# Two stacked transformer blocks on one core: what stands at the borders of stages, and on which engine

## The chip, the cores and the metric

The kernel runs on one core of a Trainium2 chip. The metric is device time in microseconds of one whole launch. The engines named below are TensorE (PE: products; its weight loads are PEld), VectorE (DVE), ScalarE (ACT), GpSimd (POOL) and SyncE (SP, which issues the weights' transfers here). Each engine works through its own list of instructions in order.

## The reference, cut to what matters

The input is one sequence of 512 tokens with 1024 features. A block of two layers is followed by a second block. Every stage has the same frame: a norm over the features, a mixer or a feed-forward, a residual.

```python
def first_block(x, c, ...):
    cond = jax.nn.silu(c)
    for layer in range(2):
        mod = cond @ ada_w[layer] + ada_b[layer]
        sh1, sc1, g1, sh2, sc2, g2 = jnp.split(mod, 6, axis=-1)
        h = modulate(rms_norm(x), sh1, sc1)          # rms_norm(x) * (1 + sc) + sh
        y = pool_attention_mixer(h, ...) if layer % 2 == 0 else mlstm_mixer(h, ...)
        x = x + g1[:, None, :] * y
        h = modulate(rms_norm(x), sh2, sc2)
        x = x + g2[:, None, :] * swiglu(h, ffn_w1[layer], ffn_w3[layer], ffn_w2[layer])
    return x
```

The second block goes on with x: `x + 0.5 * swiglu_2(rmsnorm(x))` (ffn1), a mixer of two kinds of heads (mixer2), attention of 4 heads to 256 memory rows, which have a norm, keys and values of their own (mem), `x + 0.5 * swiglu_2(rmsnorm(x))` again (ffn2), and a last norm with gains. `swiglu` is `(silu(h @ w1) * (h @ w3)) @ w2` with 2816 hidden features.

## The kernel before, in words

**Data.** x lies transposed, as 8 tiles of 128 features x 512 tokens. Every product is made in three passes of a short float format: a value is split into a high half (`wh`, `xh`) and the rest (`wl`, `xl`), and `mm3` (L160 to L162) adds wh·xh, wh·xl and wl·xh. A product here is one such pass, 128x128 by 128x512 or 128x256.

**Weights.** A block of 128 output columns comes by DMA into `raw` (SyncE, pool `rp`, two buffers of 256 columns). ScalarE copies it to `wh` (L151), VectorE subtracts to get `wl` (L130). The pool `wp` holds two `wh` and two `wl`, so at most two blocks are prepared at any time; a third waits until the products have finished with the first.

**A projection** (`proj`) goes over 8 output tiles: 8 steps of 3 products each fill one PSUM tile, then `evac` adds it to x (`resid`, L824, or L819 and L820 where the norm's factor is still to be applied), and `ss_add` squares the new tile (ScalarE) and adds it to `ssq` (GpSimd, L300 and L302). Behind the eighth tile two products with a matrix of ones (L305, L306) sum over the partitions, and `rsqrt` makes `rstd` from that: Ln and Exp on ScalarE, then four VectorE operations of a Newton step (L322 to L325).

**The norm's use.** In the first block the tiles x·(1+sc) are made ahead (`mod_pre`, GpSimd, L431). Once `rstd` is there, `modulated` (L441 to L443) multiplies by it, adds the shift and splits; `modulated_forms` (L452) does the same and goes on to the sums that the feed-forward of layer 1 needs. Four of the eight multiplications are on GpSimd (`modpool`), four on VectorE. In the second block rstd is applied to the results instead, so the products need not wait for it.

**The feed-forwards** `ffn` (layer 1, ffn1, ffn2) work in three groups of 8, 8 and 6 hidden tiles. A group is a row of units, each with seven 128x256 products per step (`uprod` 1 to 7, L562 to L564), made of sums of blocks of the weights (`usums`, `ublocks`, `usums2` on VectorE: L530, L531, L547, L548) and of x (`lead`, `trail`, L502). A unit gives gated values `g`. At the end of a group the 8 output tiles are computed from the group's `g`. Tile 0's products with the values that exist already, and then tile 1's, are issued ahead of those with the last two values, which are just being made; they fill that time. `ffn_plain` (layer 0) is the ordinary form. `mem_kv` makes keys and values of the memory (L250 to L252 or L160 to L162) at three borders: half of the keys behind pool attention's projection, half behind ffn0, the values behind the mLSTM's projection.

**Order.** A scheduler lays the program out on the engines by the order in the code, by dependences and by when buffers come free in its own estimate; what it decides is fixed before the run.

## Time and profile before

| | us |
|---|---|
| median of 3 runs (lowest, highest) | 2502.51 (2501.54, 2503.48) |
| the profiled execution, its own time | 2500.92 |
| its span in the trace | 2498.9 |
| PE busy | 2391.6 |
| DVE busy | 1832.5 |
| ACT busy | 1170.7 |
| POOL busy | 331.7 |
| mean granted clock of PE | 0.985 |

The span is the time from the first to the last instruction in the trace. Busy times are sums over instructions, and matmuls are pipelined, so a busy PE isn't yet a PE at its full pace. The granted clock says which share of full speed the chip let PE have: 1.00 is 2.4 GHz, 0.50 is 1.2.

### The profile page before, as it was taken

The numbers are of one execution on the slowest core, as the hardware profiler recorded it, in microseconds if no ns is written. First come the engines' busy times: TensorE is split into PE (matmuls) and PEld (weight loads), VectorE is DVE, ScalarE is ACT, GpSimd is POOL, SyncE is SP. The second block draws the span as 40 slices with busy tenths as digits, with TensorE's granted clock in tenths as the row PEclk, the third lists the DMA queues.
The fourth block names the chain that finished last, engine by engine and source line by source line (L and its number), as shares of the span: only waits on it lengthen the run. The fifth ranks groups of instructions, "written<-read, shape, count | busy, mean of one in ns | idle before, by whom it ended". The sixth has DMA issues, their size and how long they took to land.

```text
span 2498.9 us, 35096 instructions
## 1 busy us (share of the span) xinstructions
PE 2391.6 (96%) x13914; PEld 2068.8 (83%) x13914; DVE 1832.5 (73%) x2914; ACT 1170.7 (47%) x1880; POOL 331.7 (13%) x364
## 2 busy tenths in 40 slices
PE   7898999999999998999998999999999999999997
PEld 5567788888788668989898999988888787889896
DVE  6888765746777758857579777775778756978786
ACT  3562322222457736535366444444555545645453
POOL 1334100002212341000001000011011401000003
PEclk9999999999999999999999999999999999999999
DMA  9417564634333224333322333322111221233332
GB/s 297 132 58 229 160 219 132 212 112 152 98 112 97 82 85 127 110 101 103 101 86 85 102 102 102 102 92 84 51 51 51 85 87 58 93 102 102 102 98 72
DMA packets 265852, 276.25 MB, mean 111 GB/s; under 512 B 6588, under 2 KB 258364, under 8 KB 265688
## 3 DMA queue, kind: packets, MB, share of 16 engines
q1 hardware_dynamic: 265688, 274.02, 34.4%
q8 instruction: 109, 1.79, 0.3%
q14 instruction: 55, 0.45, 0.1%
HBM read 268.47 MB, written 5.53 MB: 110 GB/s over the span
## 4 chain that ended last, share of the span: by engine, by line
PE 73%; DVE 15%; ACT 5%; issue 4%; DMA 2%; POOL 1%; DVEq 0%; SPq 0%; ACTq 0%; POOLq 0%
PE ps L160 13%; PE ps L162 13%; PE ps L161 13%; PE ps L562 9%; PE ps L564 9%; PE ps L563 9%; DVE wl L130 2%; ACT wh L151 1%; DVE acc L388 1%; DVE qk L1059 1%; DMA rb<-rd 1%; PE ps L250 1%; PE ps L252 1%; PE ps L251 1%; DVE u L502 1%
## 5 line engine op out<-in xcount | busy, mean ns | idle before, releaser
L151 ACT ACTIVATE wh<-raw 128x1024 fp32r<-128x1024 f32 (+1 forms) x326 | 336.1, 1032 | 663.7 <-PE ps L161 488.7
L130 DVE TENSOR_TENSOR wl<-raw,wh 128x1024 fp32r<-128x1024 f32 (+1 forms) x326 | 404.8, 1242 | 72.2 <-ACT wh L151 67.4
L160 PE MATMUL ps<-h,wh 128*128 128x512 f32 x1040 | 417.9, 404 | 2.6 <-ACT wh L151 1.6
L162 PE MATMUL ps<-h,wl 128*128 128x512 f32 x1040 | 409.4, 395 | 6.6 <-DVE wl L130 6.6
L161 PE MATMUL ps<-h,wh 128*128 128x512 f32 x1040 | 412.1, 397 | 1.5 <-DVE h L852 1.2
L162 PE MATMUL ps<-g,wl 128*128 128x512 f32 (+1 forms) x780 | 297.4, 381 | 8.9 <-DVE wl L130 8.9
L160 PE MATMUL ps<-g,wh 128*128 128x512 f32 (+1 forms) x780 | 299.1, 383 | 4.5 <-DVE x L824 2.4
L161 PE MATMUL ps<-g,wh 128*128 128x512 f32 (+1 forms) x780 | 295.7, 379 | 0.0
L162 PEld LDWEIGHTS ps<-h,wl 128*128 128x128 f32 x1040 | 196.7, 189 | 52.9 <-DVE wl L130 9.1
L160 PEld LDWEIGHTS ps<-h,wh 128*128 128x128 f32 x1040 | 197.6, 190 | 45.8 <-ACT wh L151 3.6
L161 PEld LDWEIGHTS ps<-h,wh 128*128 128x128 f32 x1040 | 197.3, 190 | 45.1 <-DVE h L852 2.9
L563 PE MATMUL ps<-h,wh 128*128 128x256 f32 x726 | 206.4, 285 | 0.0
L151 ACT ACTIVATE c<-ps 128x256 f32<-128x256 f32 (+1 forms) x288 | 108.6, 385 | 172.7 <-PE ps L564 161.6
L162 PEld LDWEIGHTS ps<-g,wl 128*128 128x128 f32 x780 | 148.2, 190 | 40.7 <-DVE wl L130 14.0
L160 PEld LDWEIGHTS ps<-g,wh 128*128 128x128 f32 x780 | 148.4, 190 | 32.9 <-issue 4.3
L562 PE MATMUL ps<-h,wh 128*128 128x256 f32 x594 | 169.9, 286 | 3.1 <-ACT h L151 1.8
L161 PEld LDWEIGHTS ps<-g,wh 128*128 128x128 f32 x780 | 148.3, 190 | 28.0 <-issue 1.5
L564 PE MATMUL ps<-h,wl 128*128 128x256 f32 x594 | 168.6, 284 | 0.0
L388 DVE SCALAR_TENSOR_TENSOR acc<-araw,cond,acc 128x256 f32<-128x256 f32 x315 | 154.3, 508 | 5.4
L300 POOL COPY ssq<-sq 128x512 f32<-128x512 f32 x8 | 7.7, 958 | 1108.8 <-ACT sq L151 1108.8
L563 PEld LDWEIGHTS ps<-h,wh 128*128 128x128 f32 x726 | 140.5, 194 | 0.3 <-issue 0.2
L562 PE MATMUL ps<-hx,wh 128*128 128x256 f32 x462 | 132.8, 288 | 2.2 <-ACT wh L151 2.0
(451 smaller groups left out, 5690.6 us busy)
## 6 DMA issues: line engine op xcount, KB each, us to landing
raw<-in_ffn_w_dram SPq DMA_DIRECT2D x60, 1024.0 KB, 5.3
araw<-in_ada_w_dram SPq DMA_DIRECT2D x48, 1024.0 KB, 5.2
raw<-in_ffn_w_gu_dram SPq DMA_DIRECT2D x44, 1024.0 KB, 5.1
raw<-in_ffn_w_down_dram SPq DMA_DIRECT2D x16, 1024.0 KB, 5.1
raw<-in_w_in_dram SPq DMA_DIRECT2D x14, 1024.0 KB, 5.0
raw<-in_od_w_in_dram SPq DMA_DIRECT2D x12, 1024.0 KB, 5.5
raw<-in_mem_w_kv_dram SPq DMA_DIRECT2D x8, 1024.0 KB, 6.9
raw<-in_ffn_w_dram SPq DMA_DIRECT2D x8, 768.0 KB, 4.4
```

Source lines behind the costliest of these rows:

```text
L130: nc.vector.tensor_tensor(out=lo, in0=src, in1=hi.bitcast(F32), op=ALU.subtract)
L151: r = nc.scalar.activation(out=out, in_=in_, func=func, **kw)
L160: mm(out, wh, xh, start=first, stop=False)
L161: mm(out, wh, xl, start=False, stop=False)
L162: mm(out, wl, xh, start=False, stop=last)
L250: mm(out, xh[:, sl], wh[:, k], start=(half == 0 and i % 2 == 0 and k == 0), stop=False)
L251: mm(out, xl[:, sl], wh[:, k], start=False, stop=False)
L252: mm(out, xh[:, sl], wl[:, k], start=False, stop=(half == 1 and i % 2 == 1 and k == 3))
L388: nc.vector.scalar_tensor_tensor(out=acc, in0=tk, scalar=self.cond[:, k:k + 1], in1=acc, op0=ALU.mult, op1=ALU.add)
L562: mm(out, wh[:, k], xh, start=(m in (1, 5) and k == 0), stop=False, skip_group_check=True)
L563: mm(out, wh[:, k], xl, start=False, stop=False, skip_group_check=True)
L564: mm(out, wl[:, k], xh, start=False, stop=(k == 3), skip_group_check=True)
```

## The change

It has five parts. (1) GpSimd's work at the borders moves: the additions to `ssq` to VectorE (the first square is written there directly by ScalarE), `mod_pre`, the gains of the last norm and the high halves of the memory rows to ScalarE, the four multiplications with `rstd` to VectorE. (2) The two products with ones and `rsqrt` become `ss_fin` and are issued later: behind the first tile of `mem_kv`, behind product 1 of the first unit of a feed-forward, inside the first tiles of mixer2 and of the memory's queries. (3) The next stage's first weights are loaded and split beside the projection ahead: `unit_steps` and `weight_steps` hang on the tiles of that projection; the first unit of each group has a raw buffer of its own, `ur`. (4) `mem_kv` becomes a generator that is issued in turns with `modulated` or `modulated_forms` (`beside`). (5) At the end of a group tile 1 is issued ahead with 3 steps instead of `gn - 2`.

```diff
-    modpool, outpool = (2, 4, 5, 7), (1, 3)
+    outpool = (1, 3)
...
+    def begin(self, w, c0, ncol, step):
+
+        if step == 0:
+            self.eraw = self.raw(w, 0, KT, c0, ncol)
+        else:
+            self.esplit = self.wsplit(self.eraw[:, :, 0:P])
+
+    def raw(self, w, k0, nk, c0, ncol, t=None):
+
+        if self.esplit and self.eraw is not None:
+            v, self.eraw = self.eraw, None
+            return v
+        if t is None:
+            t = self.rp.tile([P, 2048], F32, tag="raw", name=self.nm("raw"))
         v = t[:, 0:nk * ncol].rearrange("p (k c) -> p k c", k=nk)
         self.nc.sync.dma_start(
...
     def wsplit(self, v):
+        if self.esplit:
+            v, self.esplit = self.esplit, None
+            return v
...
     def ss_add(self, src):
 
-        nc = self.nc
-        w = src.shape[-1]
-        sq = self.np.tile([P, S], F32, tag="sq", name=self.nm("sq"), bufs=3)[:, 0:w]
-        self.act(out=sq, in_=src, func=AF.Square)
         n = self.ssn
         self.ssn += 1
         if n == 0:
-            self.ssq = self.np.tile([P, S], F32, tag="ssq", name=self.nm("ssq"))[:, 0:w]
-            nc.gpsimd.tensor_copy(out=self.ssq, in_=sq)
-        elif n < KT - 1:
-            nc.gpsimd.tensor_tensor(out=self.ssq, in0=self.ssq, in1=sq, op=ALU.add)
-        if n == KT - 1:
-            self.ssp = self.ps("ss")
-            nc.tensor.matmul(self.ssp[:, 0:w], self.tab("ones"), self.ssq, start=True, stop=False)
-            nc.tensor.matmul(self.ssp[:, 0:w], self.tab("ones"), sq, start=False, stop=True)
-            self.rstd = self.rsqrt(self.ssp[:, 0:w], 1.0 / D, self.np, "rstd")
+            self.ssq = self.np.tile([P, S], F32, tag="ssq", name=self.nm("ssq"))
+            self.act(out=self.ssq, in_=src, func=AF.Square)
+            return
+        sq = self.np.tile([P, S], F32, tag="sq", name=self.nm("sq"), bufs=3)
+        self.act(out=sq, in_=src, func=AF.Square)
+        if n < KT - 1:
+            self.nc.vector.tensor_tensor(out=self.ssq, in0=self.ssq, in1=sq, op=ALU.add)
+        else:
+            self.sslast = sq
+
+    def ss_fin(self):
+
+        mm = self.nc.tensor.matmul
+        ssp = self.ps("ss")
+        mm(ssp, self.tab("ones"), self.ssq, start=True, stop=False)
+        mm(ssp, self.tab("ones"), self.sslast, start=False, stop=True)
+        self.ssn = 0
+        self.rstd = self.rsqrt(ssp, 1.0 / D, self.np, "rstd")
+        return self.rstd
...
     def mod_pre(self, layer, which, k, tag=None):
 
         pre = self.h(F32) if tag is None else self.t(tag=tag)
-        self.nc.gpsimd.tensor_scalar(out=pre, in0=self.x[k], scalar1=self.mod_cols(layer, which, k)[1], scalar2=0.0,
-                                     op0=ALU.mult, op1=ALU.add)
+        self.act(out=pre, in_=self.x[k], func=AF.Copy, scale=self.mod_cols(layer, which, k)[1])
         return pre
 
-    def modulated(self, layer, which, pres):
+    def modulated(self, layer, which, pres, hs):
+
         nc = self.nc
-        hs = []
         for k, pre in enumerate(pres):
             sh = self.mod_cols(layer, which, k)[0]
             xh, xl = self.h(), self.h()
-            (nc.gpsimd if k in self.modpool else nc.vector).tensor_tensor(out=pre, in0=pre, in1=self.rstd, op=ALU.mult)
+            nc.vector.tensor_tensor(out=pre, in0=pre, in1=self.rstd, op=ALU.mult)
             self.act(out=xh, in_=pre, func=AF.Identity, bias=sh)
             nc.vector.scalar_tensor_tensor(out=xl, in0=pre, scalar=sh, in1=xh.bitcast(F32), op0=ALU.add,
                                            op1=ALU.subtract)
             hs.append((xh, xl))
-        return hs
-
-    def modulated_forms(self, layer, which, pres):
-
-        nc, fs = self.nc, []
+            yield
...
+    def modulated_forms(self, layer, which, pres, fs):
+
         for k, pre in enumerate(pres):
-            (nc.gpsimd if k in self.modpool else nc.vector).tensor_tensor(out=pre, in0=pre, in1=self.rstd, op=ALU.mult)
+            self.nc.vector.tensor_tensor(out=pre, in0=pre, in1=self.rstd, op=ALU.mult)
             self.act(out=pre, in_=pre, func=AF.Identity, bias=self.mod_cols(layer, which, k)[0])
             if k % 2 == 0:
                 fs.append(self.lead(pre))
             else:
                 self.trail(fs[-1], pre)
-        return fs
+            yield
...
+    def unit_steps(self, us):
+
+        return lambda n: self.ubegin(us, n - 4) if n >= 4 else None
+
+    def weight_steps(self, w, c0, ncol):
+
+        return lambda n: self.begin(w, c0, ncol, n - 6) if n >= 6 else None
+
     def ubegin(self, us, step):
 
         if step == 0:
-            self.uload(us[0])
+            self.uload(us[0], True)
         elif step == 1:
             self.usums(us[0])
         elif step == 2:
             self.ublocks(us[0])
         else:
             self.uload(us[1])
-            us[0]["begun"] = True
...
+                if fresh and normed:
+                    rstd = self.ss_fin()
...
-            self.mms(ps1, t1, gs, 0, gn - 2)
-            pss = {0: (ps0, gn - 2), 1: (ps1, gn - 2)}
+            self.mms(ps1, t1, gs, 0, 3)
+            pss = {0: (ps0, gn - 2), 1: (ps1, 3)}
...
+                if then_:
+                    then_(n)
                 evac(n, ps)
-                if then_ and n >= 4:
-                    self.ubegin(then_, n - 4)
...
+        def normed():
+
+            rstd = self.ss_fin()
+            pt = self.ps("ss")
+            for c in range(4):
+                nc.tensor.transpose(pt[:, c * P:(c + 1) * P], rstd[:, c * P:(c + 1) * P], ident)
+            nc.vector.tensor_copy(out=rtok, in_=pt.rearrange("p (c d) -> p c d", c=4)[:, :, 0])
+            return rstd
...
-        self.some(side, 33)
+        self.some(side, 7)
+        rstd = normed()
+        self.some(side, 26)
...
-            self.split(self.mraw[i], self.mh[i], self.ml[i], "pool")
+        self.split(self.mraw[i], self.mh[i], self.ml[i])
...
+        tiles = self.wtiles(w, ks[0] * P, len(ks) * P) if ks else iter(())
+        nxt = next(tiles, None)
+        while nxt:
+            n, wh, wl = nxt
+            ps = self.ps("acc")
+            for k, (xh, xl) in enumerate(hs):
+                self.mm3(ps[:, 0:N], wh[:, k], wl[:, k], xh, xl, k == 0, k == KT - 1)
+            yield
+            nxt = next(tiles, None)
+            evac_k(ks[0] + n, ps)
         if vs:
+            yield from self.run_units([u for v in vs for u in self.units_tok(w, D + 256 * v, hs, evac_v(v), ntok=2)])
...
+            rstd = self.rstd if n else self.ss_fin()
...
+                if n == 7:
+                    self.some(fill, lead)
+                elif n >= 4 and layer:
+                    self.ubegin(up[0], n - 4)
                 self.resid(n, ps, self.mod[layer][:, 16 + n:17 + n])
                 self.ss_add(self.x[n])
                 pre1.append(self.mod_pre(layer, 1, n, "g" if layer else "xp"))
...
+                    self.proj(a["ev_w_out"][0], 0, D, mix, evac)
+                    self.ss_fin()
+                    self.beside(self.modulated(0, 1, pre1, ins), fill, (1, 0, 1, 0, 1, 0, 1, 0))
...
+                    fill, lead = self.mem_kv(vs=range(4)), 4
+                    self.proj(a["od_w_out"][0], 0, D, mix, evac)
+                    self.ss_fin()
+                    self.beside(self.modulated_forms(1, 1, pre1, ins), fill, (4, 4, 4, 4, 4, 4, 2, 2))
+                    self.ubegin(up[0], 3)
+                    forms, gain = [], []
+
+                    def after(n):
+                        self.gained_form(n, "ffn1_norm", forms)
+                        self.ss_add(self.x[n])
+                    self.ffn(ins, up, a["ffn_w2"][1], False, gate, after, then=self.unit_steps(up1[0]))
+                    self.ffn(forms, up1, a["ffn1_w_down_2"][0], True, 0.5, self.normed_next("mix_norm", gain),
+                             then=self.weight_steps(a["w_in_2"][0], 2048, 256))
...
+    def beside(self, g, fill, counts):
+
+        for n in counts:
+            next(g)
+            self.some(fill, n)
+        self.drain(g)
+        self.drain(fill)
...
     def normed_next(self, nxt, gain):
 
         def after(n):
-            self.ss_add(self.x[n])
             if nxt:
                 gain.append(self.gained(n, nxt))
+                self.ss_add(self.x[n])
             else:
-                self.nc.gpsimd.tensor_scalar(out=self.x[n], in0=self.x[n], scalar1=self.col("final_norm", n),
-                                             scalar2=0.0, op0=ALU.mult, op1=ALU.add)
+                self.ss_add(self.x[n])
+                self.act(out=self.x[n], in_=self.x[n], func=AF.Copy, scale=self.col("final_norm", n))
         return after
...
+    def resid_proj(self, w, mix, nxt, then, order=None, forms=None):
         gain = []
-        self.ss_start()
 
         def evac(n, ps):
+            then(n)
             self.resid(n, ps, None)
-            self.ss_add(self.x[n])
             if forms:
                 self.gained_form(n, *forms)
-                if n >= 4:
-                    self.ubegin(then, n - 4)
             else:
                 gain.append(self.gained(n, nxt))
+            self.ss_add(self.x[n])
```

**How the order moves, ffn to ffn1 on TensorE.** `ps_11555` is the last tile of the layer-1 feed-forward; L562 to L564 (L578 to L580 in the new line numbers) are products of ffn1's first unit; L305 and L306 (L320, L321) are the products with ones. Before:

```order
L160 MATMUL ps_11555<-g_11268,wh_11515 128x512
L161 MATMUL ps_11555<-g_11269,wh_11515 128x512
L162 MATMUL ps_11555<-g_11268,wl_11516 128x512
L305 MATMUL ps_11577<-ssq_11301,tabs 128x512
L563 MATMUL ps_11612<-hx_11412,w_2012_11511 128x256
L564 MATMUL ps_11612<-hx_11411,w_2013_11512 128x256
L562 MATMUL ps_11612<-h_11494,w_2012_11511 128x256
L563 MATMUL ps_11612<-h_11495,w_2012_11511 128x256
L564 MATMUL ps_11612<-h_11494,w_2013_11512 128x256
```

The second product with ones, L306, comes 12 rows behind L305. In the changed kernel the rows around the two are

```order
L578 MATMUL ps_11601<-h_11541,wh_11530 128x256
L579 MATMUL ps_11601<-h_11541,wh_11530 128x256
L580 MATMUL ps_11601<-h_11541,wl_11531 128x256
L578 MATMUL ps_11591<-h_11575,w_1998_11479 128x256
L320 MATMUL ps_11638<-ssq_11295,tabs 128x512
L579 MATMUL ps_11591<-h_11576,w_1998_11479 128x256
L580 MATMUL ps_11591<-h_11575,w_1999_11480 128x256
L321 MATMUL ps_11638<-sq_11589,tabs 128x512
L578 MATMUL ps_11591<-h_11579,wh_11530 128x256
L579 MATMUL ps_11591<-h_11580,wh_11530 128x256
L580 MATMUL ps_11591<-h_11579,wl_11531 128x256
L578 MATMUL ps_11601<-hx_11329,wh_11627 128x256
```

The last row of the layer-1 feed-forward is the one numbered 6475 of TensorE's list, L320 is number 6507: 31 products of the first unit now stand between.

**mlstm to ffn on VectorE.** `wl<-raw` are blocks of mem_kv, `nv` and `rstd` the Newton step, `g<-g,rstd` the multiplications of `modulated_forms`, `x` the residual. Before:

```order
L824 SCALAR_TENSOR_TENSOR x_92<-ps_7500,mod_85,x_92 128x512
L130 TENSOR_TENSOR wl_7576<-raw_7573,wh_7575 128x1024
L824 SCALAR_TENSOR_TENSOR x_93<-ps_7531,mod_85,x_93 128x512
L130 TENSOR_TENSOR wl_7587<-raw_7573,wh_7586 128x1024
L322 TENSOR_SCALAR nv_7565<-ps_7559 128x512
L323 TENSOR_TENSOR nv_7566<-rstd_7562 128x512
L324 TENSOR_TENSOR nv_7566<-nv_7566,nv_7565 128x512
L325 SCALAR_TENSOR_TENSOR rstd_7562<-nv_7566,rstd_7562 128x512
L130 TENSOR_TENSOR wl_7617<-raw_7614,wh_7616 128x1024
L452 TENSOR_TENSOR g_7313<-g_7313,rstd_7562 128x512
L452 TENSOR_TENSOR g_7350<-g_7350,rstd_7562 128x512
L452 TENSOR_TENSOR g_7422<-g_7422,rstd_7562 128x512
```

In the changed kernel `wl_7529<-ur` is the first block of the feed-forward's first unit:

```order
L130 TENSOR_TENSOR wl_7529<-ur_7447,wh_7528 128x1024
L312 TENSOR_TENSOR ssq_7305<-ssq_7305,sq_7537 128x512
L846 SCALAR_TENSOR_TENSOR x_93<-ps_7542,mod_85,x_93 128x512
L130 TENSOR_TENSOR wl_7570<-raw_7567,wh_7569 128x1024
L339 TENSOR_SCALAR nv_7613<-ps_7607 128x512
L340 TENSOR_TENSOR nv_7614<-rstd_7610 128x512
L341 TENSOR_TENSOR nv_7614<-nv_7614,nv_7613 128x512
L342 SCALAR_TENSOR_TENSOR rstd_7610<-nv_7614,rstd_7610 128x512
L467 TENSOR_TENSOR g_7307<-g_7307,rstd_7610 128x512
L130 TENSOR_TENSOR wl_7581<-raw_7567,wh_7580 128x1024
L467 TENSOR_TENSOR g_7344<-g_7344,rstd_7610 128x512
L130 TENSOR_TENSOR hx_7621<-g_7307,hx_7621 128x256
```

That block now stands ahead of the last tile's residual and of mem_kv's blocks (the first of them is `wl_7570`), an addition to `ssq` stands ahead of the residual, and the multiplications that GpSimd had stand in VectorE's line between the blocks. On TensorE, `wh_7528` and `wl_7529` are read from a place beside mem_kv's second block until behind its last.

**The end of the first group of the layer-1 feed-forward on VectorE.** `u`, `s`, `c` are the parts of the last gated values, `g` their splits, `wl<-raw` the output tiles' weights. Before:

```order
L130 TENSOR_TENSOR wl_8834<-sm_8740,wh_8833 128x1024
L580 TENSOR_TENSOR s_8890<-c_8849,c_8703 128x256
L130 TENSOR_TENSOR wl_8897<-raw_8894,wh_8896 128x1024
L575 TENSOR_TENSOR u_8926<-ps_8816,c_8864 128x256
L576 TENSOR_TENSOR u_8926<-ps_8816,c_8912 128x256
L621 TENSOR_TENSOR s_8812<-s_8812,u_8926 128x512
L130 TENSOR_TENSOR wl_8987<-raw_8894,wh_8986 128x1024
L130 TENSOR_TENSOR g_8931<-s_8812,g_8930 128x512
L580 TENSOR_TENSOR c_8829<-c_8946,c_8829 128x256
L642 TENSOR_TENSOR s_8890<-s_8890,c_8829 128x256
L641 TENSOR_TENSOR s_8890<-ps_8851,s_8890 128x256
L130 TENSOR_TENSOR g_8974<-s_8890,g_8973 128x512
```

In the changed kernel `ur` is the raw block of the next group's first unit and `sm` its sums:

```order
L130 TENSOR_TENSOR wl_8828<-sm_8734,wh_8827 128x1024
L596 TENSOR_TENSOR s_8884<-c_8843,c_8697 128x256
L546 TENSOR_TENSOR sm_9148<-ur_9114 128x512
L547 TENSOR_TENSOR sm_9148<-ur_9114 128x512
L130 TENSOR_TENSOR wl_8891<-raw_8888,wh_8890 128x1024
L130 TENSOR_TENSOR w_1641_9152<-sm_9148,w_1640_9151 128x1024
L130 TENSOR_TENSOR w_1648_9190<-ur_9114,w_1647_9189 128x512
L563 TENSOR_TENSOR sm_9148<-ur_9114,sm_9148 128x512
L591 TENSOR_TENSOR u_8920<-ps_8810,c_8858 128x256
L592 TENSOR_TENSOR u_8920<-ps_8810,c_8906 128x256
L564 TENSOR_TENSOR sm_9148<-ur_9114,sm_9148 128x512
L645 TENSOR_TENSOR s_8806<-s_8806,u_8920 128x512
```

Sums and splits of the next group's first unit stand between the last products' evacuations.

## Rows read from the trace of the kernel before

**Rows 1.** The page: busy time, share of the span, instructions of each engine.
```profile
PE 2391.6 (96%) x13914; PEld 2068.8 (83%) x13914; DVE 1832.5 (73%) x2914; ACT 1170.7 (47%) x1880; POOL 331.7 (13%) x364
```

**Rows 2.** Windows: stretch, length, busy PE, PEld, DVE, ACT, POOL; PEclk, DMA share, GB/s.
```profile
220.00:270.00 50.00, 42.49 (x204) 34.77 (x203) 44.32 (x64) 18.41 (x28) 18.89 (x13) 0.86 0.55 176
...
630.00:660.00 30.00, 26.04 (x145) 22.61 (x144) 23.90 (x25) 15.06 (x22) 13.35 (x12) 0.89 0.44 130
...
930.00:990.00 60.00, 51.58 (x338) 47.23 (x337) 48.93 (x70) 37.74 (x61) 12.06 (x7) 0.91 0.40 128
...
1310.00:1340.00 30.00, 22.62 (x105) 18.11 (x104) 26.79 (x42) 20.89 (x33) 9.88 (x3) 0.90 0.25 82
...
1670.00:1690.00 20.00, 16.14 (x60) 11.59 (x59) 13.92 (x28) 8.96 (x14) 3.86 (x3) 0.91 0.39 126
...
2110.00:2150.00 40.00, 35.88 (x200) 29.72 (x199) 32.00 (x48) 23.78 (x39) 6.28 (x4) 1.00 0.32 103
...
2160.00:2220.00 60.00, 60.00 (x486) 59.06 (x485) 53.46 (x86) 33.92 (x56) 0.00 (x0) 1.00 0.34 108
```

**Rows 3.** Waits of PE, whole span: total us, times, longest.
```profile
PE ps L162 <- DVE wl L130: 15.5, 13, 4.0
...
PE ps L305 <- POOL ssq L302: 8.0, 3, 3.9
```

**Rows 4.** Timeline at pool attention to ffn0: start us, us, engine; idle before in brackets.
```profile
236.14 1.21 DVE L130 TENSOR_TENSOR wl<-raw,wh 128x1024 fp32r<-128x1024 f32 x1
...
237.88 1.26 POOL L302 TENSOR_TENSOR ssq<-ssq,sq 128x512 f32<-128x512 f32 x1
...
237.94 2.29 DVE L130 TENSOR_TENSOR wl<-raw,wh 128x1024 fp32r<-128x1024 f32 x1
...
247.88 9.02 POOL L441 TENSOR_TENSOR xp<-xp,rstd 128x512 f32<-128x512 f32 x4 [7.09 <-DVE rstd L325]
...
259.23 0.80 PE L162 MATMUL ps<-h,wl 128*128 128x512 f32 x1 [3.45 <-DVE wl L130]
```

**Rows 5.** Timeline at ffn0 to mlstm.
```profile
646.87 2.28 DVE L130 TENSOR_TENSOR wl<-raw,wh 128x1024 fp32r<-128x1024 f32 x1
...
649.21 0.58 PE L162 MATMUL ps<-g,wl 128*128 128x256 f32 x1 [3.96 <-DVE wl L130]
```

**Rows 6.** Timeline at mlstm to ffn: mem_kv's first, two waiting and last two products.
```profile
935.91 0.69 PE L250 MATMUL ps<-wh,g 128*128 128x256 f32 x1
...
948.24 0.39 PE L250 MATMUL ps<-wh,g 128*128 128x256 f32 x1 [2.03 <-ACT wh L151]
...
951.03 0.39 PE L252 MATMUL ps<-wl,g 128*128 128x256 f32 x1 [2.29 <-DVE wl L130]
...
966.64 0.28 PE L251 MATMUL ps<-wh,g 128*128 128x256 f32 x1
966.76 0.28 PE L252 MATMUL ps<-wl,g 128*128 128x256 f32 x1
```

**Rows 7.** Timeline at ffn to ffn1.
```profile
1325.91 1.13 PE L305 MATMUL ps<-ssq,tabs 128*128 128x512 f32 x2 [2.68 <-POOL ssq L302]
```

**Rows 8.** Timeline at ffn1 to mixer2.
```profile
1681.85 2.06 PE L305 MATMUL ps<-ssq,tabs 128*128 128x512 f32 x2 [3.86 <-POOL ssq L302]
```

**Rows 9.** Timeline at the ends of two groups: tile 2, layer-1 ffn and ffn2.
```profile
1066.34 1.06 ACT L151 ACTIVATE wh<-raw 128x1024 fp32r<-128x1024 f32 x1 [6.24 <-PE ps L161]
...
1068.71 0.50 PE L162 MATMUL ps<-g,wl 128*128 128x512 f32 x1 [0.42 <-DVE wl L130]
...
2355.50 0.50 PE L162 MATMUL ps<-g,wl 128*128 128x512 f32 x1 [0.83 <-DVE wl L130]
```

**Rows 10.** Timeline at the end of the first group, layer-1 ffn.
```profile
1054.07 0.42 DVE L575 TENSOR_TENSOR u<-ps,c 128x256 f32<-128x256 f32 x1 [2.07 <-PE ps L564]
...
1058.81 0.40 PE L160 MATMUL ps<-g,wh 128*128 128x512 f32 x1
...
1060.13 0.69 DVE L130 TENSOR_TENSOR g<-s,g 128x512 fp32r<-128x512 f32 x1 [0.70 <-ACT g L151]
```

148 lines of the change are left out of this document (60 added, 88 removed).

## The prediction

> **What bounds the kernel now.** I read four views in this order: the busy shares, the windows by stretch, the waits of TensorE, and the timeline at each wait. The shares say that TensorE is the bound: it is busy 96% of the span, VectorE 73%, GpSimd 13% [rows 1]. So only time in which TensorE stands idle, or runs at half its clock, can be won. The windows say where that is. In a stretch inside a feed-forward stage (the last row) TensorE is busy for all 60 us at a granted clock of 1.00, although VectorE is busy for 53.5 of them. At the borders it isn't: I take for each border "length minus TensorE's busy time" as idle time, and "length times (1 minus granted clock)" as what the slow clock cost, since a stretch at half clock (1.2 of 2.4 GHz) loses half its length [rows 2]. That gives
>
> - pool attention to ffn0 (220 to 270): 7.5 + 7.0 = 14.5 us
> - ffn0 to mlstm (630 to 660): 4.0 + 3.3 = 7.3
> - mlstm to the layer-1 ffn (930 to 990): 8.4 + 5.4 = 13.8
> - ffn to ffn1 (1310 to 1340): 7.4 + 3.0 = 10.4
> - ffn1 to mixer2 (1670 to 1690): 3.9 + 1.8 = 5.7
> - mem to ffn2 (2110 to 2150): 4.1 + 0 = 4.1
>
> together 55.8 us. The waits name two culprits: the low half wl of a weight block, made on VectorE (15.5 us in 13 waits), and the sum of squares ssq, made on GpSimd, which the norm's product with a matrix of ones waits for (8.0 us in 3) [rows 3]. The timeline shows how they hang together. A wl takes 1.21 us; one that starts 0.06 us behind the start of a GpSimd add takes 2.29 [rows 4]. So GpSimd costs twice: its own chain is late, and it lengthens VectorE's work beside it by 1.1 us a time.
>
> **A rule beside that row.** The Trainium skill, "SBUF — State Buffer", section "SBUF: two separate sides", says that VectorE (with two SBUF inputs) and GpSimd hold one port pair in turn, for whole instructions, and the other one fully blocks. The pair of rows agrees with it in kind (1.08 us more, beside an add of 1.26). By the rule alone the price would be the whole of the other instruction, 1.26; the sum below goes by the rows.
>
> **The change, part by part.** *GpSimd's work at borders goes.* 109 of its 367 instructions in program order leave it; ScalarE gets 42 more, VectorE 60. At the 0.69 us that a 128x512 VectorE operation takes (the split of g in [rows 10]) that is some 41 us more for VectorE, over seven norms: 6 us a border. It lies beside TensorE's products as long as nobody waits for a wl behind it; where somebody does, each costs 0.7 us. Against it stands 1.1 us less for each operation that had a GpSimd neighbour. I count this at nothing by itself and let it show in the border terms.
>
> *The norm's products of ones move behind the first products.* At ffn to ffn1 they stand right behind the last projection tile's products, and TensorE waits 2.68 us for the add of ssq [rows 7]; at ffn1 to mixer2 it waits 3.86 us [rows 8]. In the new order 31 products of unit 0 (0.12 us each by the last two of [rows 6], 3.7 us) stand ahead of them at the first, and 21 products of the next projection (twice the columns, so some 0.23 each, 4.8 us) at the second. Both are longer than the waits. The rest of the border ffn to ffn1 is weights that were prepared after the projection instead of beside it, and the half clock behind these idle times. Of its 10.4 us I take 9: what stays is unit 1's wl, queued on VectorE behind the Newton steps, which wait for ScalarE's Exp (1 to 2 us; low end 7, high end all of it). Of ffn1 to mixer2 I take 5.5 of 5.7 (low 5). Mem to ffn2 has its norm late in the same way, but its idle time is five small waits: 3.5 of 4.1 (low 1).
>
> *The filler of a group's end.* Tile 1 gets 3 of its 8 (or 6) steps instead of 6 (or 4) before the last gated values, so 15 products instead of 6 lie between the moment at which tile 0's block comes free and tile 2's first use of wl. Tile 2's wh (1.06 us), then wl (1.21) need 2.3 us [rows 9, 4]; 6 x 0.23 = 1.4 us doesn't cover that, 15 x 0.23 = 3.4 does. There are two stalls of 0.42, four of 0.83 (where the residual takes two VectorE operations ahead of the wl) [rows 9], and three more of that kind (0.30 to 0.48) in the groups of six: 5.4 us idle and some 0.1 us at each restart, where the first product shows 0.50: 6 us (low 4.5, high 7).
>
> *The same filler shortens the cover of the gated values.* Nine products fewer, 2.1 us, stand ahead of the first product that reads them. In the row of before the last g is split by 1060.82 [rows 10]; 18 products from 1058.81 in the new order put its first use at 1062.9, its last-named at 1063.8. The next unit's preparation, now hoisted here, brings VectorE some 4.6 us, of which the 2.07 us that it idled [rows 10], and as much before, take most. I cost it at nothing; what happens when the cover is gone is the slower rival below.
>
> *The borders with mem_kv.* These three carry the doubt. At pool attention to ffn0, VectorE takes over four of the eight products with rstd (GpSimd's took 9.02 us for four [rows 4]) and the adds: about 7 us of its own in front of the first weights, against the neighbours' 1.1 us each on some eight operations, and an ssq that nobody waits for. I lay the chain out with the durations named: ffn0's first wl comes 3 us earlier, its second 5, and the wait of 3.45 us before it [rows 4] with the half clock behind it goes; a shorter stall comes back at the third block, since VectorE is then behind. I take 5 of 14.5 (2 to 7). At ffn0 to mlstm the one wait is 3.96 us for a wl of 2.28 [rows 5]; without the neighbour it is 1.1 shorter, but the norm's chain ends 2 us later, since the products of ones moved back: 1.5 (-1 to 4).
>
> At mlstm to ffn the change speaks against itself. The first block of the feed-forward is made beside the last projection tile and then keeps one of the two places for prepared weights until unit 0 has used it, which the new order shows to end behind mem_kv's last block. So the eight blocks of mem_kv pass through the one that is left: no block is prepared while the one before it is in use. A block is then wh 1.06 + wl 1.21 + 24 products of 0.12 = 5.15 us, eight are 41.2; before, the 192 products of them took from 935.91 to 967.0, 31.1 us [rows 6]. That is 10.1 us lost. Won back: the waits behind mem_kv (8.4 minus the two in it of 2.0 and 2.3 us: 4.1), two thirds of the half clock there (3.6), and 33 products of unit 0 that now stand between mem_kv's blocks (0.12 each, 4.0): 11.7, so 1.6 more than lost. I take 1. If nothing comes back it is -10; if more of that waiting overlaps, +4.
>
> **Sum.** 5 + 1.5 + 1 + 9 + 5.5 + 3.5 + 6 = 31.5 us. All low ends give 8.5, all high ends 42.2. The profiled execution took 2500.9 us, 2.0 more than its span; the median of the runs is 1.6 above it. So 2500.9 - 31.5 + 1.6 = **2471 us**, 1.3% faster. 0.2% (5 us) is about what a measurement here can tell from no change.
>
> **The rivals.**
> *All of it.* If the weights ready ahead cover the mem_kv borders too, every loss listed goes: 55.8 + 7 = 62.8 us, 2440. For it: in the steady stretch TensorE loses nothing with VectorE at 89% [rows 2]. Against: the two places for prepared weights, which the change doesn't add to. 0.1.
> *The late sums only change engines.* On VectorE the adds stand in line with wl, residual and unit sums, and the products of ones could come to wait for VectorE as they did for GpSimd. Then the two borders with long ssq waits keep their loss: 31.5 - 14.5 = 17, 2486. The Trainium skill, "TensorE: Matmul & The Clock Gate", section "Architectural detail: the array is 16x 32x32, not 1x 128x128", has VectorE and ScalarE as strict first-in-first-out queues; by it any operation that waits holds all behind it. For the rival also speaks VectorE's load at ffn to ffn1 (26.8 of 30 us [rows 2]); against it, that much of this load is the stretching by GpSimd that goes. 0.15.
> *Mem_kv at half clock.* With a gap of 2.3 us in each block at mlstm to ffn, the clock may not come back between them, as it fell behind idle times of 3.5 to 4.0 us [rows 4, 5]. A block is then 2.3 + 24 x 0.24 = 8.0 us, eight 64: 23 us more than taken, so 31.5 - 23 = 8.5 and 2494. Against it: the products of unit 0 in the gaps. 0.1.
> *Slower: the ends of groups.* If VectorE meets the gated values late by the whole of the hoisted preparation, TensorE waits at each of the nine group ends for up to 4.6 us: 41 us against 32, 2512. It decides from 3.5 us an end. For it: VectorE at 89% in ffn1 and ffn2 [rows 2], and 2 us of cover less. Against: a last unit has no successor to prepare in the old order, so the hoisted work only fills it up to what every unit carries. 0.05.
>
> **Chances and range.** The forecast 0.6, the rivals as given. The likeliest case by itself reaches from 2460 to 2488. The range of 2450 to 2490 leaves out most of the first and third rival and the slower one. Faster by over 0.2%: 0.9; within: 0.05; slower: 0.05.
>
> **What would show it.** Right: no wait for ssq anywhere; no idle time at tile 2 of a group; ffn to ffn1 and ffn1 to mixer2 at a granted clock of 1.00 with under 2 us idle each; no GpSimd operation at a border and wl at 1.2 us there; mem_kv at mlstm to ffn with some 41 us for its 192 products, and the unit behind it free of waits. Wrong: a wait for g at the ends of groups; the products of ones waiting for VectorE; mem_kv as fast as before (too low a forecast) or above 50 us (too high).

## The result, and the profile after

The changed kernel took 2474.91 us (median of 4 runs, 2470.28 to 2477.28) against 2502.21 (4 runs, 2501.54 to 2503.48): ratio 0.9888, 95% interval 0.9871 to 0.9905, so 27.3 us faster. Forecast were 2471 us and 31.5 us less, in a range of 2450 to 2490. The total came out; three of its terms did not, as the table below shows.

The profiled execution of the changed kernel is the slowest of its four (2477.28 us), 23.6 us below that of before. Its page, part 1:

```profile
PE 2386.4 (96%) x13914; PEld 2069.8 (84%) x13914; DVE 1821.5 (74%) x2973; ACT 1194.1 (48%) x1922; POOL 173.0 (7%) x255
```

GpSimd's busy time is halved against [rows 1]. VectorE has 59 instructions more and still 11 us less of busy time: what it took over (some 41 us by the prediction's estimate) is less than what it no longer loses beside GpSimd.

The windows that answer to [rows 2], in the same columns, with one more (650 to 685, the mLSTM's first products):

```profile
215.00:260.00 45.00, 39.50 (x210) 33.70 (x209) 41.79 (x74) 24.28 (x36) 0.00 (x0) 0.92 0.62 200
620.00:650.00 30.00, 26.09 (x139) 22.44 (x138) 24.42 (x37) 16.16 (x24) 0.88 (x5) 0.83 0.43 130
650.00:685.00 35.00, 31.11 (x130) 24.83 (x130) 27.14 (x38) 15.17 (x19) 0.47 (x8) 0.95 0.32 92
925.00:990.00 65.00, 53.44 (x323) 47.49 (x322) 42.74 (x68) 35.89 (x58) 0.00 (x0) 0.89 0.36 114
1300.00:1345.00 45.00, 42.79 (x254) 37.08 (x254) 41.53 (x69) 34.64 (x54) 0.00 (x0) 1.00 0.34 111
1655.00:1675.00 20.00, 20.00 (x88) 16.08 (x86) 17.70 (x38) 9.92 (x15) 0.00 (x0) 1.00 0.44 143
2090.00:2130.00 40.00, 38.66 (x222) 33.48 (x222) 34.31 (x58) 25.69 (x41) 0.00 (x0) 1.00 0.29 92
```

Read as in the prediction (idle time, plus length times what the clock lacks of 1): ffn to ffn1 loses 2.2 us where it lost 10.4, ffn1 to mixer2 nothing, mem to ffn2 1.3. The first three borders lose 5.5 + 3.6 = 9.1, 3.9 + 5.1 = 9.0 and 11.6 + 7.2 = 18.7 us. The last two are more than the 7.3 and 13.8 of before.

Who gains where can be had more closely from the two traces: TensorE works off 13914 products in both, so the start of the k-th product in one, minus its start in the other, says how far the changed kernel is ahead there. The differences between such points, beside the terms of the prediction:

| stretch (k-th product) | forecast | measured |
|---|---|---|
| start and pool attention to ffn0 (0 to 1250) | -5 | -10.0 |
| ffn0 to mlstm, with the mLSTM's start (2500 to 3250) | -1.5 | +4.0 |
| rest of the mLSTM (3250 to 4000) | 0 | +3.1 |
| mlstm to ffn (4000 to 4750) | -1 | +6.3 |
| ffn to ffn1 (6500 to 7250) | -9 | -8.4 |
| ffn1 to mixer2 (9000 to 9250) | -5.5 | -6.4 |
| mem to ffn2 (11250 to 11750) | -3.5 | -4.3 |
| ends of groups, three stages | -6 | -5.9 |
| mixer2 and mem, and behind 13750 | 0 | -1.6 |

Taken together the changed kernel is 23.2 us ahead. A minus is a gain; the k-th product need not be the same one in both, since the order differs. TensorE's waits over the whole span, to be held against [rows 3]:

```profile
PE ps L162 <- DVE wl L130: 9.6, 5, 3.1
...
PE ps L160 <- ACT wh L151: 5.7, 5, 2.4
...
PE ps L264 <- ACT wh L151: 4.3, 5, 1.0
...
PE ps L266 <- DVE wl L130: 3.3, 4, 1.2
```

No row of the view names ssq any more. The two lower rows are mem_kv's products (L264 to L266): nine of their blocks' halves came late, where two did before, by 2.0 and 2.3 us [rows 6].

### The profile page after: what moved, and what is told of

Read it like the earlier page. It is cut to its first block, busy times and chain, and to the rows that moved or that the text cites. A ratio compares the mean times of both kernels' runs of the same rounds, so it can differ in the third digit from the quotient of the medians.

```text
span 2475.6 us, 34963 instructions
## 1 busy us (share of the span) xinstructions
PE 2386.4 (96%) x13914; PEld 2069.8 (84%) x13914; DVE 1821.5 (74%) x2973; ACT 1194.1 (48%) x1922; POOL 173.0 (7%) x255
## 4 chain that ended last, share of the span: by engine, by line
PE 79%; DVE 11%; ACT 5%; DMA 2%; issue 2%; POOL 1%; SPq 0%; DVEq 0%; ACTq 0%; POOLq 0%
PE ps L160 15%; PE ps L161 15%; PE ps L162 15%; PE ps L578 9%; PE ps L580 9%; PE ps L579 9%; DVE wl L130 2%; DMA rb<-rd 1%; ACT wh L151 1%; PE ps L264 1%; PE ps L266 1%; PE ps L265 1%; DVE acc L405 1%; PE ps L424 1%; PE ps L1004 1%
## 5 line engine op out<-in xcount | busy, mean ns | idle before, releaser
L151 ACT ACTIVATE wh<-raw 128x1024 fp32r<-128x1024 f32 (+1 forms) x317 | 326.7, 1031 | 623.4 <-PE ps L161 459.6
L130 DVE TENSOR_TENSOR wl<-raw,wh 128x1024 fp32r<-128x1024 f32 (+1 forms) x317 | 388.5, 1226 | 61.1 <-ACT wh L151 56.4
L160 PE MATMUL ps<-h,wh 128*128 128x512 f32 x1040 | 418.5, 404 | 6.8 <-ACT wh L151 5.7
L162 PE MATMUL ps<-h,wl 128*128 128x512 f32 x1040 | 410.8, 397 | 8.3 <-DVE wl L130 8.3
L160 PE MATMUL ps<-g,wh 128*128 128x512 f32 (+1 forms) x780 | 296.7, 380 | 0.0
L162 PE MATMUL ps<-g,wl 128*128 128x512 f32 (+1 forms) x780 | 295.4, 379 | 1.3 <-DVE wl L130 1.3
L162 PEld LDWEIGHTS ps<-h,wl 128*128 128x128 f32 x1040 | 197.5, 190 | 55.0 <-DVE wl L130 10.8
L160 PEld LDWEIGHTS ps<-h,wh 128*128 128x128 f32 x1040 | 197.8, 190 | 49.7 <-ACT wh L151 7.9
L162 PEld LDWEIGHTS ps<-g,wl 128*128 128x128 f32 x780 | 147.8, 190 | 28.9 <-DVE wl L130 1.7
L578 PE MATMUL ps<-h,wh 128*128 128x256 f32 x594 | 168.4, 283 | 3.1 <-ACT c L151 3.1
L160 PEld LDWEIGHTS ps<-g,wh 128*128 128x128 f32 x780 | 147.8, 190 | 27.1 <-issue 0.5
L580 PE MATMUL ps<-h,wl 128*128 128x256 f32 x594 | 168.1, 283 | 0.0
L846 DVE SCALAR_TENSOR_TENSOR x<-ps,mod,x 128x512 f32<-128x512 f32 x64 | 47.9, 750 | 117.5 <-PE ps L162 117.5
L578 PE MATMUL ps<-hx,wh 128*128 128x256 f32 x462 | 130.9, 284 | 1.9 <-ACT hx L151 1.4
```

The source lines that it names most:

```text
L130: nc.vector.tensor_tensor(out=lo, in0=src, in1=hi.bitcast(F32), op=ALU.subtract)
L151: r = nc.scalar.activation(out=out, in_=in_, func=func, **kw)
L160: mm(out, wh, xh, start=first, stop=False)
L162: mm(out, wl, xh, start=False, stop=last)
L578: mm(out, wh[:, k], xh, start=(m in (1, 5) and k == 0), stop=False, skip_group_check=True)
L580: mm(out, wl[:, k], xh, start=False, stop=(k == 3), skip_group_check=True)
```

## The experiments

All twelve were timed against the kernel before, four or five runs each.

| kernel | median us | ratio, 95% interval |
|---|---|---|
| the changed kernel | 2474.9 | 0.9888, 0.9871 to 0.9905 |
| e1, first block behind mem_kv | 2460.3 | 0.9829, 0.9815 to 0.9842 |
| e2, filler back | 2475.4 | 0.9885, 0.9872 to 0.9899 |
| e3, before with the filler alone | 2494.8 | 0.9967, 0.9955 to 0.9980 |
| e4, sums back on GpSimd | 2486.5 | 0.9933, 0.9919 to 0.9946 |
| e5, products of ones first | 2473.4 | 0.9881, 0.9867 to 0.9894 |
| e6, before with the engines alone | 2471.4 | 0.9865, 0.9850 to 0.9880 |
| e7, e1 and mem_kv in one piece | 2458.7 | 0.9820, 0.9807 to 0.9834 |
| e8, before with the sums alone | 2484.7 | 0.9926, 0.9914 to 0.9939 |
| e9, before, engines and filler | 2463.7 | 0.9848, 0.9834 to 0.9861 |
| e10, e1 with no unit begun ahead | 2460.6 | 0.9835, 0.9822 to 0.9849 |
| e11, e1, ones first, mem_kv in one piece | 2456.7 | 0.9819, 0.9805 to 0.9832 |
| e12, e10 without the raw buffer `ur` | 2473.6 | 0.9893, 0.9877 to 0.9910 |

**e1: the held place.** Theory: at mlstm to ffn the block that is made ahead holds one of two places, and mem_kv goes through the other. Rival: the multiplications that VectorE took over delay mem_kv's blocks.

```diff
-                elif n >= 4 and layer:
+                elif 4 <= n < 6 and layer:
                     self.ubegin(up[0], n - 4)
...
                     self.beside(self.modulated_forms(1, 1, pre1, ins), fill, (4, 4, 4, 4, 4, 4, 2, 2))
+                    self.ubegin(up[0], 2)
                     self.ubegin(up[0], 3)
```

> The changed kernel with one thing undone: at mlstm to ffn the first block of the feed-forward's first unit is split behind mem_kv instead of ahead of it (its load and its sums stay ahead). If the held place for prepared weights is what made this border lose, mem_kv's 192 products take 30 to 34 us again instead of some 47, a wait of 2 to 4 us for that block comes back behind them, and the median falls by 4 to 9 us to 2466 to 2471. If the multiplications that VectorE took over from GpSimd are the cause, mem_kv stays above 42 us and the time within 3 us of 2475.

14.6 us faster than the changed kernel, more than expected; by the k-th products (4000 to 4750) this border goes from 6.3 us lost to 8.9 won. The wait behind mem_kv that was expected to come back is 1.3 us and not 2 to 4. In the changed kernel mem_kv's first and last product and three of its blocks stand like this in the timeline (start, duration, idle time before in brackets):

```profile
934.79 0.36 PE L264 MATMUL ps<-wh,g 128*128 128x256 f32 x1 [0.16 <-issue]
...
964.72 1.06 ACT L151 ACTIVATE wh<-raw 128x1024 fp32r<-128x1024 f32 x1 [2.03 <-PE ps L265]
...
965.82 1.23 DVE L130 TENSOR_TENSOR wl<-raw,wh 128x1024 fp32r<-128x1024 f32 x1 [1.53 <-ACT wh L151]
...
969.92 1.06 ACT L151 ACTIVATE wh<-raw 128x1024 fp32r<-128x1024 f32 x1 [3.09 <-PE ps L265]
...
971.00 1.23 DVE L130 TENSOR_TENSOR wl<-raw,wh 128x1024 fp32r<-128x1024 f32 x1 [2.76 <-ACT wh L151]
...
972.29 0.39 PE L266 MATMUL ps<-wl,g 128*128 128x256 f32 x1 [0.76 <-DVE wl L130]
...
975.10 1.06 ACT L151 ACTIVATE wh<-raw 128x1024 fp32r<-128x1024 f32 x1 [2.23 <-PE ps L265]
...
981.14 0.41 PE L266 MATMUL ps<-wl,g 128*128 128x256 f32 x1
```

The chain is closed: ScalarE waits for the products (L265) of the block before, VectorE for ScalarE, TensorE for VectorE, and none of them is busy meanwhile. (The first turns are different: from 935 to 948 us VectorE is busy for 9.9 of 13 us, and the granted clock is 0.74.) That also speaks against the rival, by which VectorE would be late for work of its own: it idles 2.76 us before a split. A turn takes 969.92 - 964.72 = 5.2 us, all of mem_kv 46.8 where it took 31.1 [rows 6]. In e1 the same products, and the window around them:

```profile
931.51 0.28 PE L264 MATMUL ps<-wh,g 128*128 128x256 f32 x1
...
960.42 0.28 PE L266 MATMUL ps<-wl,g 128*128 128x256 f32 x1
```

```profile
922.00:985.00 63.00, 58.47 (x423) 54.17 (x422) 52.87 (x84) 43.24 (x73) 0.00 (x0) 1.00 0.44 136
```

29.2 us, at a full clock; VectorE does all of the multiplications here too and is busier (52.9 of 63 us) than in the changed kernel (42.7 of 65). The border loses 4.5 us instead of 18.7.

**e2 and e3: the filler.** One puts the filler back in the changed kernel, the other puts it alone into the kernel before:

```diff
-            self.mms(ps1, t1, gs, 0, gn - 2)
-            pss = {0: (ps0, gn - 2), 1: (ps1, gn - 2)}
+            self.mms(ps1, t1, gs, 0, 3)
+            pss = {0: (ps0, gn - 2), 1: (ps1, 3)}
```

> The changed kernel with tile 1's filler back at gn - 2 steps. If the shorter filler is what removed the stalls at tile 2, nine stalls of 0.3 to 0.8 us come back and the median rises by 5 to 7 us to 2480 to 2482. If the stalls went because of VectorE's new order, nothing changes: 2473 to 2477.

> The kernel before with the filler of 3 steps alone. If the filler is worth 6 us by itself, the median is 2495 to 2497. If it takes cover from the gated values even without the hoisted preparation, TensorE waits for g at the group ends and the time is 2500 or more.

Alone the filler is worth 2503.97 - 2494.76 = 9.2 us (the ratio's interval: 5 to 11). By the k-th products 3.8 us of this come at the ends of groups in the three stages and 3.7 at ffn to ffn1, where e3's wait for ssq is 1.4 us instead of 2.7. In the changed kernel the filler is worth nothing that the times show; by the k-th products e2 loses 0.7 us in each of the three stages, 2.1 in all. The timeline of TensorE in e2 at the place of [rows 9] shows why the stall doesn't come back:

```profile
1068.16 0.39 PE L160 MATMUL ps<-g,wh 128*128 128x512 f32 x1
1068.38 0.39 PE L161 MATMUL ps<-g,wh 128*128 128x512 f32 x1
1068.61 0.28 PE L578 MATMUL ps<-hx,w 128*128 128x256 f32 x1
1068.72 0.28 PE L579 MATMUL ps<-hx,w 128*128 128x256 f32 x1
1068.85 0.28 PE L580 MATMUL ps<-hx,w 128*128 128x256 f32 x1
1069.19 0.50 PE L162 MATMUL ps<-g,wl 128*128 128x512 f32 x1
```

Three products of the next group's first unit (L578 to L580), whose weights lie ready, stand in the place where TensorE waited for tile 2's wl. The filler and the unit prepared ahead mend the same stall; either is enough for it, and e2's three stages show no row of TensorE waiting.

**e6 and e8: the engines.** e6 is the kernel before with additions, multiplications, `mod_pre` and splits on the new engines, and everything in the old order; e8 moves the sums alone:

```diff
-        self.act(out=sq, in_=src, func=AF.Square)
...
+        if n:
+            self.act(out=sq, in_=src, func=AF.Square)
         if n == 0:
...
-            nc.gpsimd.tensor_copy(out=self.ssq, in_=sq)
+            self.act(out=self.ssq, in_=src, func=AF.Square)
         elif n < KT - 1:
-            nc.gpsimd.tensor_tensor(out=self.ssq, in0=self.ssq, in1=sq, op=ALU.add)
+            nc.vector.tensor_tensor(out=self.ssq, in0=self.ssq, in1=sq, op=ALU.add)
```

> The kernel before with the engines changed alone: additions to ssq and the multiplications with rstd on VectorE, mod_pre, the gains of the last norm and the high halves of the memory rows on ScalarE; every order in the code as before. If GpSimd's late sums and its stretching of VectorE's work are worth as much as the waits for ssq and half of the first border, the median is 2485 to 2492. If the 41 us more on VectorE eat that up, or the products of ones now wait for VectorE, it is 2499 to 2506.

> The kernel before with the sums of squares alone moved from GpSimd to VectorE (the first square written by ScalarE). If the sums are the larger part of what the engines gave, the three waits for ssq (8.0 us) and the half clock behind them go and the median is 2485 to 2492. If it is the multiplications with rstd and mod_pre, it is 2496 or more.

The sums alone give 18.8 us, the most that was expected of them. The engines together give 32.6, far beyond the expectation and at least as much as the whole change with its 27.3 (the two intervals overlap). Which of the other moves gives the 13.8 us between e8 and e6 no run separates. The waits of e6:

```profile
PE ps L162 <- DVE wl L130: 7.8, 8, 2.2
```

15.5 us in 13 waits were in [rows 3]; the waits for ssq are gone with the products of ones in their old place.

**e4: the sums back.** The changed kernel with `self.nc.gpsimd` for `self.nc.vector` in `ss_add`.

> The changed kernel with the six additions to ssq of every norm back on GpSimd; the products of ones stay behind the first products. If the late sums cost through the wait of the products of ones alone, the moved products hide them and the median stays at 2473 to 2478. If GpSimd costs through stretching VectorE's splits beside it, the waits for wl grow at the borders and the median is 2482 or more.

11.6 us slower, so the second theory has the time. Its sign didn't come as named: TensorE's waits for wl (L162) fall from 9.6 to 7.0 us, and those for wh (L160) and h (L578) grow by 2.7 and 2.5. No product of ones of the borders waits for ssq (one row of 0.2 us, in the last norm): the late sums are hidden, as the first theory has it, and the time is lost all the same. By the k-th products e4 is 4.4 us behind the changed kernel at pool attention to ffn0, 4.3 at ffn to ffn1 and 1.1 at mem to ffn2. The second of these can be followed. Grouped by form, the sums and differences of 128x256 there are in e4

```profile
L517 DVE TENSOR_TENSOR u<-u,u 128x256 f32<-128x256 f32 x8 | 6.4, 800 | 0.1
```

and in the changed kernel

```profile
L517 DVE TENSOR_TENSOR u<-u,u 128x256 f32<-128x256 f32 x8 | 3.3, 418 | 0.0
```

In e4's timeline they stand beside GpSimd's additions, ahead of the last tile's residual (L846):

```profile
1321.08 1.61 POOL L312 TENSOR_TENSOR ssq<-ssq,sq 128x512 f32<-128x512 f32 x1 [2.97 <-ACT sq L151]
1321.12 1.85 DVE L517 TENSOR_TENSOR u<-u,u 128x256 f32<-128x256 f32 x2
...
1326.26 1.46 POOL L312 TENSOR_TENSOR ssq<-ssq,sq 128x512 f32<-128x512 f32 x1 [3.57 <-ACT sq L151]
...
1326.49 1.51 DVE L130 TENSOR_TENSOR h<-s,h 128x256 fp32r<-128x256 f32 x1
...
1327.92 0.74 DVE L846 SCALAR_TENSOR_TENSOR x<-ps,mod,x 128x512 f32<-128x512 f32 x1
...
1331.18 0.58 PE L578 MATMUL ps<-h,w 128*128 128x256 f32 x1 [2.15 <-ACT h L151]
...
1331.78 1.91 PE L320 MATMUL ps<-ssq,tabs 128*128 128x512 f32 x2
```

and in the changed kernel the last split and the residual are

```profile
1320.42 0.42 DVE L130 TENSOR_TENSOR h<-s,h 128x256 fp32r<-128x256 f32 x1
...
1321.36 0.74 DVE L846 SCALAR_TENSOR_TENSOR x<-ps,mod,x 128x512 f32<-128x512 f32 x1
```

The residual starts 0.1 us behind the end of its tile's products in the changed kernel and 3.0 us behind it in e4. Three places at which VectorE's operation stands beside an addition (the two shown, and one at 1317.01 us) make some 3 us of that. The h for which TensorE then waits 2.15 us is made from this tile, by operations that take 0.41 us again. That wait stands ahead of the product of ones, which itself waits for nothing. So GpSimd's addition costs by what it does to its neighbour on VectorE: 0.42 us become 0.80 on the mean. The Trainium skill, "SBUF — State Buffer", section "SBUF: two separate sides", has a VectorE operation with two SBUF inputs and a GpSimd operation that reads SBUF exclude each other for whole instructions. The 0.80 beside 0.42 agrees with it in kind. e4 also has another order in places, since the scheduler lays each program out anew, so its 11.6 us are not all shown to come from this stretching.

**e5, e7, e11: where the norm and mem_kv stand.** e5 puts the products of ones right behind each projection again; e7 is e1 with mem_kv's products all ahead of the multiplications at the first two borders; e11 has both. The edits at one place each, first e5's, then e7's:

```diff
+                if fresh and normed:
+                    rstd = self.ss_fin()
                 if fresh:
                     for m in (5, 1, 2):
...
                     self.ss_fin()
+                    self.drain(fill)
                     self.beside(self.modulated(0, 1, pre1, ins), fill, (1, 0, 1, 0, 1, 0, 1, 0))
```

> The changed kernel with the products of ones right behind the last tile of each projection again (and mem_kv's first steps behind them), sums on VectorE. If the engine of the sums is what counted, as the kernel with the engines alone suggests, the median stays within 3 us of 2475. If the position counts, waits of 1 to 3 us for ssq or sq come back at five borders and it is 2481 or more.

> The kernel of e1_block_behind_kv, and at the first two borders mem_kv's products all issued ahead of the multiplications with rstd instead of in turns with them. If the turns make ffn0 to mlstm slower than before (it lost some 4 us), that border gains 3 to 5 us and the median is 2455 to 2458. If the products with their weights in one piece leave VectorE idle for the norm and the norm's chain then lies open, it is 2462 or more.

> The kernel of e1_block_behind_kv with the products of ones right behind each projection and mem_kv in one piece ahead of the multiplications at the first two borders: engines, filler and weights ahead are what is left of the change. If norms behind the first products and the turns with mem_kv are worth nothing, the median is 2456 to 2462. If they hide the norm's chain, it is 2465 or more.

e5 measures as the changed kernel (0.9881 beside 0.9888), e7 as e1 (0.9820 beside 0.9829), e11 lowest of all but inside e7's and e1's intervals. By the times, neither the place of the products of ones nor the turns with mem_kv can be told from nothing, once the sums are on VectorE. The traces show a little for the place: at ffn to ffn1 e5 and e11 win 7.0 us by the k-th products where the changed kernel wins 8.4. Both wait there for a value of ScalarE, which costs the changed kernel 0.4 us (e5, 1290 to 1345 us):

```profile
PE ps L578 <- ACT c L151: 3.1, 1, 3.1
```

**e9: engines and filler.** The edits of e6 and e3 together.

> The kernel before with two parts, the engines and the filler of 3 steps; weights, norms and mem_kv in the old order. If the two add up as they measured apart (33 and 9 us), the median is 2460 to 2464, and the rest of the change, without the held place, gives next to nothing more. If the filler gave its 9 us only where GpSimd stretched the splits, it is 2468 to 2472.

2463.7: they add up nearly (32.6 and 9.2 apart, 38.4 together). Two parts in the old order are thus 11 us faster than all five. They are 3 us slower than e1, within the intervals of both.

**e10 and e12: what is prepared ahead.** e10 takes the calls out of the projections' tiles:

```diff
-        return lambda n: self.ubegin(us, n - 4) if n >= 4 else None
+        return lambda n: None
...
+            if not us[0].get("begun"):
+                for step in range(4):
+                    self.ubegin(us, step)
             tiles = self.wtiles(w2, 0, D, j0, gn)
```

> The kernel of e1_block_behind_kv with no unit of a feed-forward begun ahead: load, sums and blocks of each group's first unit behind the group before it. If what stands ready gave the 6.5 us at ffn to ffn1, 2.6 at mem to ffn2 and some at the group ends that the kernel with the engines alone lacks, the median rises by 9 to 12 us to 2469 to 2473. If the engines gave them, it stays within 3 us of 2460.

2460.6, as e1: the order on TensorE and VectorE turned out the same, row by row. The experiment was built wrongly for its question, and is a second timing of e1. e12 also takes the buffer away:

```diff
-            self.uload(us[0], True)
+            self.uload(us[0])
```

> e10_e1_none_ahead turned out to be laid out by the scheduler in the very order of e1_block_behind_kv, instruction by instruction on TensorE and VectorE: with a raw buffer of its own the first unit's load and sums are taken ahead wherever the code has them. Here that buffer goes too, so the first unit of a group waits for one of the two common ones, and its load, sums and blocks come behind the output tiles' own. If weights ready ahead are worth what ffn to ffn1, mem to ffn2 and the group ends got beyond the kernel with the engines alone, some 10 us, the median is 2467 to 2473. If only the engines and the filler count, it stays within 3 us of 2460.

13.0 us slower than e10. By the k-th products, e12 is behind e1 by 7.5 us at mlstm to ffn and by 4.0 at ffn to ffn1. At the first, the held place is back in another pool: the load of the unit's raw block still stands ahead of mem_kv and now keeps one of the two common raw buffers. Mem_kv's loads go through the other, its blocks come in pairs some 10 us apart, and its products take 40.0 us:

```profile
939.67 1.06 ACT L151 ACTIVATE wh<-raw 128x1024 fp32r<-128x1024 f32 x1 [1.63 <-DMA raw<-in_mem_w_kv_dram]
...
941.16 1.06 ACT L151 ACTIVATE wh<-raw 128x1024 fp32r<-128x1024 f32 x1
...
950.27 1.06 ACT L151 ACTIVATE wh<-raw 128x1024 fp32r<-128x1024 f32 x1 [0.84 <-DMA raw<-in_mem_w_kv_dram]
```

So a load ahead needs the raw buffer of its own; where the code calls for the load is the scheduler's to overrule (e10). What the two are worth against the old order isn't shown by e12: e9, which has neither this buffer nor a load ahead of mem_kv, is only 3 us behind e1.

## Why the prediction was right, and where it was not

**The sum** of 31.5 us was near the 27.3 measured, partly by luck, because errors cancel: 5 us too little at the first border, 5.5 and 7 too much at the next two, 3 us of the mLSTM that aren't the change's.

**Ends of groups, ffn to ffn1, ffn1 to mixer2, mem to ffn2:** 6, 9, 5.5 and 3.5 were forecast; 5.9, 8.4, 6.4 and 4.3 came. The sizes are right; the reasons given are right for one of three. The products of ones behind the first products were to hide the waits for ssq, and at ffn to ffn1 the profile after shows them without a wait:

```profile
1325.02 1.02 PE L320 MATMUL ps<-ssq,tabs 128*128 128x512 f32 x2
...
1326.11 1.02 PE L321 MATMUL ps<-sq,tabs 128*128 128x512 f32 x2
```

But e6 has no waits for ssq either, with them in the old place, and e5 loses nothing in time and 1.4 us there by the k-th products. The step that failed is "I count this at nothing by itself": the engines' move is not a carrier for the other parts, it is the larger part, 32.6 us by itself. At ffn1 to mixer2 e6 gets 6.1 us, the changed kernel 6.4. At ffn to ffn1 e6 gets 2.2 of the 8.4. Most of the rest is weights ready ahead, which the prediction named: without the raw buffer 4.0 us of it go (e12), with the products of ones first 1.4 (e5). At the ends of groups the filler alone gets 3.8 us of the 6 computed (e3) and the weights ahead without it 3.8 as well (e2), so the 5.9 are the work of two remedies and not of the filler. Ffn to ffn1 kept 2.2 us of idle time, where the prediction named under 2 as a sign of being right.

**Pool attention to ffn0:** 5 of 14.5 were forecast, 10.0 came (8.0 to 11.9 in e1, e2, e10 and e12, which have the same order here), 2.7 of it ahead of the 750th product. The mis-sized step is "about 7 us of its own in front of the first weights, against the neighbours' 1.1 us each on some eight operations": e6 gets 11.2 here, and e8, with the sums alone, 8.0. The waits that remain (timeline):

```profile
245.36 1.06 ACT L151 ACTIVATE wh<-raw 128x1024 fp32r<-128x1024 f32 x1 [1.04 <-DMA raw<-in_ffn_w_dram]
...
246.47 0.50 PE L160 MATMUL ps<-h,wh 128*128 128x512 f32 x1 [2.42 <-ACT wh L151]
...
250.27 0.79 PE L162 MATMUL ps<-h,wl 128*128 128x512 f32 x1 [3.08 <-DVE wl L130]
```

The first hangs on the block's transfer, which lands only at 245.3. The prediction expected VectorE to be behind at the third block; the wl of the first wait's block is late as well (3.08 us), at 250.22.

**ffn0 to mlstm:** -1.5 was forecast, +4.0 came in the profiled execution. Five kernels (the changed one, e1, e2, e10, e12) have the same order up to this border, and over the same products (2500 to 3250) e1 and e12 lose 0.2 us each, e2 loses 2.8 and e10 gains 0.3. So the same instructions give anything from about nothing to 4 us lost, and the 4.0 go in part with the clock of this one execution (below). The gain that was forecast came in none of them; e6, with mem_kv in the old order, gains 2.3 here. What is given back within the stage is seen in the timeline of the changed kernel:

```profile
678.30 0.80 PE L162 MATMUL ps<-h,wl 128*128 128x512 f32 x1 [2.36 <-DVE wl L130]
```

A wait for a wl comes 30 us behind the border, where VectorE's line has the gates' scans ahead of it; the like of it cost 0.48 us before, and in the same order 0.83 in e1 and 2.35 in e12. The prediction's step "without the neighbour it is 1.1 shorter" looked at the border alone. The 3.1 us in the rest of the mLSTM are not the change: e3, with before's order there, is 3.3 behind the profiled execution of before over nearly the same products.

**mlstm to ffn:** -1 was forecast, +6.3 came. The mechanism was right, and so was its turn: 5.15 us forecast, 5.1 to 5.3 in four of the seven turns from block to block. Two sizes were off. Mem_kv took 46.8 us and not 41.2, since the other three turns took 8.1, 5.9 and 6.7: unit 0's products stand in the gaps, and around the longest (935 to 948 us) the clock was 0.74. And the 11.7 us that were to be won back came as 9.4: 46.8 - 31.1 = 15.7 lost against 6.3 net. I had weighed this as one of three doubtful borders, while e1 shows it to be the most costly thing in the change: 14.6 us. Of the rivals, "mem_kv at half clock" came nearest to this (the window's clock is 0.89).

**The rivals.** "The late sums only change engines" did not come: no wait for ssq or for VectorE's additions. "Slower: the ends of groups" did not come: there is no wait for g there. "All of it" did not come in this change, and e11, at 2456.7, gets 45 of those 63 us.

**A better version.** e11 is the fastest measured, 18.2 us below the changed kernel, with e7, e1 and e10 within 4 us of it: engines, filler and the raw buffer kept, the first block of the unit split behind mem_kv in the code. Engines and filler alone (e9) are 7 us behind it.

## What to carry to other kernels

A block prepared ahead holds its place until it is used; where the work that runs meanwhile passes through the same pool, count the places left, since two places overlap preparation with use and one does not (here for split weights in the changed kernel, for raw blocks in e12). An operation on an engine with time to spare can cost more than it takes if it slows the neighbour that the bound engine waits for; moving it to the busy neighbour was here the largest gain. Before crediting a change of order in the source, compare the orders that the scheduler makes of it, and test parts that mend the same stall separately and together.
